# Two modulation vectors against 33.6 MB of weights: the weights become the stationary side of f32 products

## The chip, the core and the metric

One core of a Trainium2 chip runs the whole program, two transformer blocks on 256 tokens of width 2048. The metric is the device time in microseconds (us), the median of three runs; lower is better.

## What is computed

Only the start of the first block is touched by the change. Two vectors, `c` of the latent tokens and `c_ctx` of the context tokens, pass through silu and are multiplied by one matrix; the three parts of the result shift, scale and gate the block.

```python
c_act = jax.nn.silu(c)
cc_act = jax.nn.silu(c_ctx)
mod_lat = c_act @ w_ada[l] + b_ada[l]      # w_ada: 2048 x 6144, f32
mod_ctx = cc_act @ w_ada[l] + b_ada[l]
shift_l, scale_l, gate_l = jnp.split(mod_lat, 3, axis=-1)
u_l = rms_norm(h_lat, pre_w) * (1 + scale_l[:, None]) + shift_l[:, None]
u_c = rms_norm(h_ctx, pre_w) * (1 + scale_c) + shift_c
z_l, xbc_l, dt_l, qkv_l, b_l, a_l = _split_proj(u_l @ w_in)
```

Everything after that (two scans, gating, an output projection, then two layers of attention, convolution and MLP) is left as it is.

## The kernel before

The program is recorded by Python generators; a scheduler then orders the instructions of each engine, and each engine runs its own list strictly in that order. All activations stand feature-major: 128 features on the partitions, tokens along the free side.

Precision is the theme of the code. A product of two f32 numbers is made from float32r operands: `split` (lines 168 to 171) has ScalarE (ACT) write the rounded value `hi` and VectorE (DVE) the rest `lo`, and TensorE adds hi times hi, hi times lo and lo times hi. An operand that isn't split goes to TensorE as plain f32; the trace then shows two MATMUL records, each with a weight load (LDWEIGHTS), for one f32 product in the code.

The modulation runs first. `ada_prepare` (line 319) makes silu of both vectors (`cth`) and splits it (`cst`, 4 columns for each of 16 slices of 128 rows). `ada(m0, ...)` (line 331) makes four tiles of 128 outputs. For each of the 16 row slices it loads 128 x 512 weights (256 KB) on SyncE's DMA queue, splits them, and issues two products with `cst` as the stationary side (4 columns) and the weights moving (512 columns), once for `hi` and once for `lo`. At the end it copies the 4 x 512 result to SBUF, turns it with four transposes, and adds the parts and the bias into `modT` with two additions.

`block1_inputs` (line 390) drives this. For j = 0 to 3 it calls `ada` for four tiles of scale and then for four tiles of shift: eight calls, 128 weight tiles, 33.6 MB. The last third of `w_ada` (the gate) is done much later by `ada_gate`, in another way, from `cth`. Beside the calls, `along` (line 417) runs a side generator at every third step: during j = 0 it loads the 256 tokens of both sides and sums their squares on TensorE (16 f32 products of 512 columns); from j = 1 on it runs the first projections, 32 steps of 12 float32r products of 256 columns each. The eight steps of a j need the u tiles that its shift call completes, so the eight steps of j = 3 come after the last modulation. `small` (line 465) follows, with four transposes as its first work on TensorE.

The tile pools set how far loads run ahead: the split weights take their buffers from `RINGS` (line 1353), raw tiles from tags tok, kT and Am, `hi` from A and hs, `lo` from U and W.

Of the kernel before, what the change touches and what calls it, by code (L numbers as in the profile page):

```python
# [11 lines left out]
F32 = mybir.dt.float32  # L12
FR = mybir.dt.float32r
I32 = mybir.dt.int32
AF = mybir.ActivationFunctionType
ALU = mybir.AluOpType
# [6 lines left out]
NK = D // 128  # L23
# [8 lines left out]
class Kern:  # L32
# [286 lines left out]
    def ada_prepare(self):  # L319
        cv = self.cvec.rearrange("p (k t) -> p k t", t=2)  # L320
        th = self.lt([128, NK, 2], "cth")
        self.act(th, cv, AF.Tanh, scale=0.5)
        self.stt(th, th, 1.0, cv, ALU.add, ALU.mult)
        self.tsc(th, th, 0.5, ALU.mult)
        st = self.lt([128, NK, 4], "cst", FR)
        self.split(th, st[:, :, 0:2], st[:, :, 2:4])
        self.cst, self.cth, self.nada = st, th, 0
        self.modT = self.lt([128, 48, 2], "modT")
        self.wada = iter([self.a["w_ada"][i] for i in range(96)])

    def ada(self, m0, bank, rings):


        ps = self.pt([4, 512], bank)
        for kb in range(8):
            ap = next(self.wada)
            for kk in range(2):
                k = 2 * kb + kk
                i = self.nada = self.nada + 1
                raw, hi, lo = (self.m([128, 512], t[i % len(t)], dt) for t, dt in zip(rings, (F32, FR, FR)))  # L340
                self.nc.sync.dma_start(out=raw, in_=ap[:, kk * 512:kk * 512 + 512])
                self.split(raw, hi, lo)
                self.mm(ps, self.cst[:, k, :], hi, start=(k == 0), stop=False)
                self.mm(ps, self.cst[:, k, :], lo, start=False, stop=(k == NK - 1))
            if kb < 7:
                yield 1.4
        res = self.m([4, 512], "cc")
        self.act(res, ps)
        pm = self.pt([128, 4, 4], "pt")
        for t in range(4):  # L350
            self.transpose(pm[:, t, :], res[:, t * 128:t * 128 + 128])
        m = self.modT[:, m0:m0 + 4, :]
        self.tt(m, pm[:, :, 0:2], self.b_ada[:, m0:m0 + 4].unsqueeze(2).to_broadcast([128, 4, 2]), ALU.add)
        self.tt(m, m, pm[:, :, 2:4], ALU.add)
        yield 1.4

    def ada_gate(self, m0):
# [32 lines left out]
    def block1_inputs(self, early, got):  # L390

        nc = self.nc
        xs, r = [], []

        def first():
            ps = self.pt([128, 512], "pg")
            for j in range(4):
                if j < 2:
                    t = self.t8([128, 2, 4, T])
                    x = [t[:, 0], t[:, 1]]  # L400
                else:
                    x = [self.xt(), self.xt()]
                for s in range(2):
                    nc.sync.dma_start(out=x[s], in_=self.a["xc"][j, s])
                xs.append(x)
                yield
                for k in range(4 * j, 4 * j + 4):
                    sq = self.m([128, 2, T], "src")
                    for s in range(2):
                        self.act(sq[:, s], x[s][:, k % 4, :], AF.Square)  # L410
                    self.mm(ps, self.ones, sq.rearrange("p s t -> p (s t)"), start=(k == 0), stop=(k == NK - 1))
                yield
            q, x, t = (self.m([128, 512], "X"), self.m([128, 512], "g"), self.m([128, 512], "g"))
            self.rsqrt(q, ps, 1.0 / D, EPS, x, t)
            r.append(q)

        def along(m0, side):
            for i, dt in enumerate(self.ada(m0, "pc", RINGS)):
                if i % PUMP == 0:
                    next(side, None)  # L420
                yield dt

        self.u = [], []
        self.u_lat = self.pick(self.u[1])
        self.u_full = lambda k: (self.pick(self.u[0])(k), self.pick(self.u[1])(k))
        steps = []
        psc = self.lt([128, NK, 2], "psc")
        side = first()
        for j in range(4):
            yield from along(16 + 4 * j, side)  # L430
            if not j:
                for _ in side:
                    pass
                for i in range(0, len(early), 2):
                    ps = [self.acc([128, 1, 512]) if t == "acc" else self.pt([128, 1, 512], t) for t in early[i:i + 2]]
                    got += ps
                    steps.append(self.proj_steps(self.win, 2, self.u_full, 512, ps=ps, fine=True))
            m = slice(4 * j, 4 * j + 4)
            self.stt(psc[:, m, :], self.modT[:, 16 + 4 * j:20 + 4 * j, :], 1.0,
                     self.pre_w[:, m].unsqueeze(2).to_broadcast([128, 4, 2]), ALU.add, ALU.mult)  # L440
            for s in range(2):
                for k in range(4):
                    x, f = xs[j][s][:, k, :], 4 * j + k
                    self.stt(x, x, psc[:, f, s:s + 1], r[0][:, s * T:s * T + T], ALU.mult, ALU.mult)
            yield from along(4 * j, side)
            for _ in side:
                pass
            for s in range(2):
                u = self.t8([128, 2, 4, T], FR)
                for k in range(4):  # L450
                    x, f = xs[j][s][:, k, :], 4 * j + k
                    sh = self.modT[:, f, s:s + 1]
                    self.act(u[:, 0, k, :], x, AF.Identity, bias=sh)
                    self.stt(u[:, 1, k, :], x, sh, u[:, 0, k, :].bitcast(F32), ALU.add, ALU.subtract)
                self.u[s].append(u)
            side = (next(p) for p in steps for _ in range(4))
        for _ in side:
            pass
# [891 lines left out]
COPY = ("W", "W", "Am")  # L1350
EARLY = ("acc", "acc", "pA", "pg")
SHARE = 0
RINGS = (("tok", "tok", "kT", "tok", "Am"), ("A", "A", "hs"), ("U", "U", "W"))
SIDE0, SIDE, SIDK = 0, 2, (0,)
HEADS = range(0, 40, 5)
SHZ = 0
# [137 lines left out]
```

## Time and profile before

| | us |
|---|---|
| median of 3 runs | 3246.17 (3239.31 to 3249.16) |
| the profiled execution | 3253.82 |
| its span in the trace | 3252.0 |
| TensorE busy in the span | 3139.1 (97%) |
| VectorE busy | 2084.6 (64%) |
| ScalarE busy | 1538.7 (47%) |

A profile is of one execution. TensorE has two rows: PE is the matmuls, PEld the weight loads that run beside them. "Busy" is the union of an engine's instructions, and a matmul's record lasts longer than the time until the next can start, so a busy TensorE can still have room; the time that one matmul costs in a row of them is the distance from start to start. PEclk is the granted clock of TensorE, 1.00 for 2.4 GHz and 0.50 for 1.2 GHz. An average over 3.2 ms says nothing of the first 171 us, so the stretch is read by itself.

### The profile page before, as it was taken

What the parts mean: (1) busy time and instruction counts of PE and PEld (TensorE: products, weight loads), DVE (VectorE), ACT (ScalarE), POOL (GpSimd) and SP (SyncE); (2) the same over time, 40 slices, a digit from 0 to 9 for tenths busy, and PEclk for the clock granted to TensorE, in tenths of its full rate; (3) what the DMA queues carried; (4) which work ended last, traced back from release to release, by engine and by line L of the source; (5) the groups of instructions that cost most, each with busy time, mean ns of one, the idle gap of its engine ahead of it and who ended that gap; (6) DMA issues with size and microseconds to landing.
All of it is one profiled execution on the core that took longest, in us unless ns stands there. A gap on an engine that the chain in (4) does not pass through costs nothing.

```text
span 3252.0 us, 50361 instructions
## 1 busy us (share of the span) xinstructions
PE 3139.1 (97%) x19370; PEld 2730.0 (84%) x19370; DVE 2084.6 (64%) x3552; ACT 1538.7 (47%) x2290; POOL 530.5 (16%) x290
## 2 busy tenths in 40 slices
PE   7889999997989998999999999999999999999999
PEld 3589999987977887888888888888888888888888
DVE  7878988988756566555555554655765555555555
ACT  6654435453444455444444444444554544444443
POOL 0000000000002221322222222222213222222221
PEclk9999999998999999999999999999999999999999
DMA  9634432443764554565556565665546565555655
GB/s 319 229 105 118 125 102 86 114 112 117 249 236 153 166 180 136 186 187 188 182 189 187 188 185 185 188 189 159 179 159 186 185 189 185 185 188 186 191 184 181
DMA packets 217537, 565.75 MB, mean 174 GB/s; under 512 B 45808, under 2 KB 69856, under 8 KB 217296
## 3 DMA queue, kind: packets, MB, share of 16 engines
q1 hardware_dynamic: 214976, 555.72, 54.4%
q0 software_dynamic: 1456, 4.65, 0.4%
q8 instruction: 152, 2.49, 0.3%
q10 hardware_dynamic: 864, 2.16, 0.2%
q14 instruction: 89, 0.73, 0.1%
HBM read 552.83 MB, written 9.63 MB: 173 GB/s over the span
## 4 chain that ended last, share of the span: by engine, by line
PE 84%; DVE 5%; DMA 5%; ACT 2%; issue 1%; POOL 1%; SPq 0%; DVEq 0%; ACTq 0%; POOLq 0%
PE acc L146 76%; PE p_pc L146 3%; PE p_pg L146 2%; PE ps L146 2%; DVE lo L130 1%; DMA W<-w_ada 1%; DMA raw<-w_in 1%; ACT hi L143 1%; PE p_pA L146 1%; POOL lo L130 1%; DMA Am<-w_ada 1%; DMA A<-rows 1%; DVE t L133 1%; ACT t L143 0%; DMA t<-bias 0%
## 5 line engine op out<-in xcount | busy, mean ns | idle before, releaser
L146 PE MATMUL acc<-t,hi 128*128 128x512 f32 (+1 forms) x7552 | 2174.7, 356 | 18.7 <-ACT t L143 8.1
L146 PE MATMUL acc<-t,lo 128*128 128x256 f32 x6080 | 1659.3, 285 | 23.6 <-DVE lo L130 21.6
L143 ACT ACTIVATE hi<-raw 128x1024 fp32r<-128x1024 f32 x906 | 960.6, 1060 | 1337.3 <-PE acc L146 597.8
L146 PEld LDWEIGHTS acc<-t,hi 128*128 128x128 f32 x7552 | 1304.3, 190 | 232.6 <-DVE t L133 11.3
L146 PEld LDWEIGHTS acc<-t,lo 128*128 128x128 f32 x6080 | 1127.6, 190 | 51.3 <-DVE lo L130 26.8
L130 DVE TENSOR_TENSOR lo<-raw,hi 128x1024 fp32r<-128x1024 f32 x714 | 874.6, 1225 | 460.3 <-PE acc L146 383.6
L130 POOL TENSOR_TENSOR lo<-raw,hi 128x1024 fp32r<-128x1024 f32 x192 | 462.8, 2410 | 1874.9 <-PE acc L146 1621.8
L146 PE MATMUL acc<-c,hi 128*128 128x512 f32 x1280 | 459.5, 396 | 0.1
L146 PE MATMUL acc<-c,lo 128*128 128x256 f32 x1280 | 358.8, 280 | 0.0
L130 DVE TENSOR_TENSOR x<-x,acc 128x512 f32<-128x512 f32 x288 | 197.5, 686 | 215.5 <-PE acc L146 212.8
L146 PEld LDWEIGHTS acc<-c,hi 128*128 128x128 f32 x1280 | 240.4, 188 | 51.3 <-DVE t L130 0.4
L130 DVE TENSOR_TENSOR t<-t,acc 128x512 f32<-128x512 f32 x104 | 71.3, 687 | 296.4 <-ACT t L143 296.4
L146 PEld LDWEIGHTS acc<-c,lo 128*128 128x128 f32 x1280 | 241.5, 189 | 3.9
L133 DVE SCALAR_TENSOR_TENSOR cc<-src,featv,cc 128x248 f32<-128x248 f32 (+2 forms) x224 | 98.7, 470 | 0.3 <-ACT cc L143 0.2
L146 PE MATMUL acc<-hi,t 128*128 128x512 f32 x256 | 80.3, 393 | 0.0
L146 PE MATMUL ps<-t,t 128*128 128x128 f32 (+2 forms) x320 | 62.9, 340 | 10.7 <-ACT t L143 10.6
L133 DVE SCALAR_TENSOR_TENSOR t<-t,t 128x1024 f32<-128x1024 f32 (+2 forms) x68 | 62.4, 918 | 2.0
L146 PEld LDWEIGHTS ps<-t,t 128*128 128x128 f32 (+1 forms) x320 | 43.1, 180 | 23.5 <-ACT t L143 14.0
L143 ACT ACTIVATE t<-t 128x1024 f32<-128x1024 f32 (+1 forms) x56 | 59.3, 1059 | 6.4 <-DVE t L130 3.4
L130 DVE TENSOR_TENSOR t<-t,t 128x512 f32<-128x512 f32 (+2 forms) x64 | 60.4, 943 | 0.9
L725 POOL MEMSET W<- 64x256 f32 x16 | 4.9, 308 | 340.6 <-PE p_pg L146 268.0
L143 ACT ACTIVATE t<-acc 128x512 f32<-128x512 f32 x104 | 60.3, 582 | 0.0
(318 smaller groups left out, 2360.9 us busy)
## 6 DMA issues: line engine op xcount, KB each, us to landing
raw<-w_in SPq DMA_DIRECT2D x298, 512.0 KB, 3.8
raw<-w_up SPq DMA_DIRECT2D x256, 512.0 KB, 4.2
raw<-w_down SPq DMA_DIRECT2D x256, 512.0 KB, 3.8
raw<-w_out SPq DMA_DIRECT2D x96, 512.0 KB, 4.4
tok<-w_ada SPq DMA_DIRECT2D x77, 256.0 KB, 5.1
Am<-w_ada SPq DMA_DIRECT2D x57, 256.0 KB, 3.7
W<-w_ada SPq DMA_DIRECT2D x32, 256.0 KB, 3.4
kT<-w_ada SPq DMA_DIRECT2D x26, 256.0 KB, 5.9
```

Of the source, the lines that this page charges most:

```text
L130: return (eng or self.nc.vector).tensor_tensor(out=out, in0=in0, in1=in1, op=op)
L133: (eng or self.nc.vector).scalar_tensor_tensor(out=out, in0=in0, scalar=s, in1=in1, op0=op0, op1=op1)
L143: self.nc.scalar.activation(out=out, in_=in_, func=func, **kw)
L146: return self.nc.tensor.matmul(out, lhsT, rhs, start=start, stop=stop, skip_group_check=skip)
L725: nc.gpsimd.memset(W[jp], 0.0)
```

## The change

The weights are used as they arrive, in plain f32, as the stationary side: four products per weight tile, each with 128 columns of it, and the two vectors moving (2 columns). The result lies feature-major at once, in one PSUM bank of 128 x 4 x 2. The splits of the weights and of `cth`, the copy, the transposes and the second addition are gone. The raw tiles now rotate through one list of 23 buffers made of all the tags that raw, hi and lo had.

```diff
-        st = self.lt([128, NK, 4], "cst", FR)
-        self.split(th, st[:, :, 0:2], st[:, :, 2:4])
-        self.cst, self.cth, self.nada = st, th, 0
+        self.cth, self.nada = th, 0
...
-    def ada(self, m0, bank, rings):
+    def ada(self, m0):
-        ps = self.pt([4, 512], bank)
+        ps = self.pt([128, 4, 2], "pc")
         for kb in range(8):
             ap = next(self.wada)
             for kk in range(2):
                 k = 2 * kb + kk
-                i = self.nada = self.nada + 1
-                raw, hi, lo = (self.m([128, 512], t[i % len(t)], dt) for t, dt in zip(rings, (F32, FR, FR)))
+                raw = self.m([128, 512], RING[self.nada % len(RING)])
+                self.nada += 1
                 self.nc.sync.dma_start(out=raw, in_=ap[:, kk * 512:kk * 512 + 512])
-                self.split(raw, hi, lo)
-                self.mm(ps, self.cst[:, k, :], hi, start=(k == 0), stop=False)
-                self.mm(ps, self.cst[:, k, :], lo, start=False, stop=(k == NK - 1))
+                for t in range(4):
+                    self.mm(ps[:, t, :], raw[:, t * 128:t * 128 + 128], self.cth[:, k, :], start=k == 0 and t == 0,
+                            stop=k == NK - 1, skip=True)
             if kb < 7:
                 yield 1.4
-        res = self.m([4, 512], "cc")
-        self.act(res, ps)
-        pm = self.pt([128, 4, 4], "pt")
-        for t in range(4):
-            self.transpose(pm[:, t, :], res[:, t * 128:t * 128 + 128])
-        m = self.modT[:, m0:m0 + 4, :]
-        self.tt(m, pm[:, :, 0:2], self.b_ada[:, m0:m0 + 4].unsqueeze(2).to_broadcast([128, 4, 2]), ALU.add)
-        self.tt(m, m, pm[:, :, 2:4], ALU.add)
+        self.tt(self.modT[:, m0:m0 + 4, :], ps, self.b_ada[:, m0:m0 + 4].unsqueeze(2).to_broadcast([128, 4, 2]), ALU.add)
         yield 1.4
...
-RINGS = (("tok", "tok", "kT", "tok", "Am"), ("A", "A", "hs"), ("U", "U", "W"))
+RING = ("tok", "A", "U", "kT", "tok", "hs", "W", "A", "tok", "U", "Am", "kT", "tok", "A", "U", "tok", "hs", "W", "kT", "A",
+        "tok", "U", "Am")
```

TensorE's list in the third pair of calls, before. `p_pc` is the modulation's sum, A, hs and U, W the split weights; `p_pA` and `p_pg` are two of the early projections' sums, `t` their u tiles.

```order
L146 MATMUL p_pg_342<-t_240_901,hi_0_1187 128x256 x2
L146 MATMUL p_pg_342<-t_241_910,hi_0_1187 128x256 x2
L146 MATMUL p_pg_342<-t_240_901,lo_0_1188 128x256
L146 MATMUL p_pc_1108<-W_1205,cst 4x512
L146 MATMUL p_pc_1108<-A_1212,cst 4x512
L146 MATMUL p_pg_342<-t_241_910,lo_0_1188 128x256
L146 MATMUL p_pA_341<-t_240_901,hi_0_1187 128x256 x2
L146 MATMUL p_pc_1108<-U_1213,cst 4x512
L146 MATMUL p_pc_1108<-A_1220,cst 4x512
L146 MATMUL p_pA_341<-t_241_910,hi_0_1187 128x256 x2
L146 MATMUL p_pA_341<-t_240_901,lo_0_1188 128x256
L146 MATMUL p_pc_1108<-U_1221,cst 4x512
```

The scheduler wove single modulation products between the projection's. In the changed program, the same engine in the second pair of calls (an f32 product is one row here):

```order
L146 MATMUL p_pc_905<-cth,A_984 128x2 x4
L146 MATMUL p_pc_905<-cth,tok_990 128x2 x4
L146 MATMUL p_pc_905<-cth,U_996 128x2 x4
L146 MATMUL p_pc_905<-cth,Am_1002 128x2 x4
L146 MATMUL p_pc_905<-cth,tok_1008 128x2 x4
L146 MATMUL p_pc_905<-cth,A_1014 128x2 x4
L146 MATMUL p_pA_298<-t_104_738,hi_0_968 128x256 x2
L146 MATMUL p_pA_298<-t_105_747,hi_0_968 128x256 x2
L146 MATMUL p_pA_298<-t_104_738,lo_0_969 128x256
L146 MATMUL p_pA_298<-t_105_747,lo_0_969 128x256
L146 MATMUL p_pg_299<-t_104_738,hi_0_968 128x256 x2
L146 MATMUL p_pg_299<-t_105_747,hi_0_968 128x256 x2
```

Now the list alternates between six weight tiles (24 products of two columns) and one step of 12 projection products.

VectorE's list in the first half of the modulation, before:

```order
L130 TENSOR_TENSOR U_561<-kT_559,A_560 128x512
L130 TENSOR_TENSOR W_569<-tok_567,hs_568 128x512
L130 TENSOR_TENSOR modT<-p_pt_483,featv 128x8
L130 TENSOR_TENSOR U_577<-Am_575,A_576 128x512
L130 TENSOR_TENSOR U_585<-tok_583,A_584 128x512
L130 TENSOR_TENSOR W_605<-tok_603,hs_604 128x512
L130 TENSOR_TENSOR U_613<-kT_611,A_612 128x512
L130 TENSOR_TENSOR modT<-modT,p_pt_483 128x8
```

and in the changed program, from the first to the third pair of calls:

```order
L133 SCALAR_TENSOR_TENSOR t_66_407<-t_6_118,modT,t_66_407 128x256 x4
L133 SCALAR_TENSOR_TENSOR t_67_416<-t_6_118,modT,t_67_416 128x256 x4
L130 TENSOR_TENSOR modT<-p_pc_425,featv 128x8
L133 SCALAR_TENSOR_TENSOR psc<-modT,featv 128x8
L133 SCALAR_TENSOR_TENSOR t_23_209<-t_23_209,psc,X_281 128x256 x8
L130 TENSOR_TENSOR lo_0_772<-raw_769,hi_0_771 128x1024
L130 TENSOR_TENSOR modT<-p_pc_574,featv 128x8
L133 SCALAR_TENSOR_TENSOR t_104_738<-t_23_209,modT,t_104_738 128x256 x4
```

The splits stood between all other work of VectorE; now only the u tiles, the bias additions and the projection weights' splits are left there.

## Rows read from the trace of the kernel before

**Rows 1.** The page, head and busy time (share of the span, instructions)
```profile
span 3252.0 us, 50361 instructions
PE 3139.1 (97%) x19370; PEld 2730.0 (84%) x19370; DVE 2084.6 (64%) x3552; ACT 1538.7 (47%) x2290; POOL 530.5 (16%) x290
```

**Rows 2.** Windows: stretch, its length, engines' busy us (instructions), PEclk, DMA share, GB/s
```profile
0.00:171.00 171.00, 143.17 (x709) 79.69 (x709) 127.29 (x244) 113.81 (x219) 1.22 (x6) 0.93 0.78 263
```

**Rows 3.** The chain of waits, five pieces of 89 to 171 us: start, us, what
```profile
89.53 6.23 DMA tok<-w_ada
...
120.76 1.30 DVE U L130 x2
...
157.16 0.18 DVE modT L130
...
160.46 1.48 PE acc L146 x12
...
170.58 0.39 PE p_pt L150 x4
```

**Rows 4.** Timeline of modulation steps: start, us, engine, line, what [idle before, releaser]
```profile
6.30 0.63 ACT L143 ACTIVATE A<-tok 128x512 fp32r<-128x512 f32 x1 [1.36 <-DMA tok<-w_ada]
...
15.60 0.63 PE L146 MATMUL p_pc<-U,cst 128*4 128x512 f32 x1
...
90.03 0.68 DVE L130 TENSOR_TENSOR U<-tok,A 128x512 fp32r<-128x512 f32 x1
...
153.70 0.40 PE L146 MATMUL p_pc<-U,cst 128*4 128x512 f32 x1
153.93 0.39 PE L146 MATMUL p_pc<-hs,cst 128*4 128x512 f32 x1
```

**Rows 5.** The tile p_pc over the whole span: duration ns min/median/max, first and last start
```profile
L146 PE MATMUL p_pc<-gV,gK x96: 271/275/580, 454.0 to 832.0; 128*128 128x128 f32 x96
```

**Rows 6.** Timeline at 1117 us, two f32 products with one moving column (line 1321's helper)
```profile
1117.76 0.52 PEld L146 LDWEIGHTS ps<-consts,t 1*128 1x128 f32 x4 [0.35 <-PE acc L146]
1117.76 0.60 PE L146 MATMUL ps<-consts,t 1*128 1x1 f32 x4
```

**Rows 7.** Groups of weight loads by form: count | busy us, mean ns of one | idle before
```profile
L146 PEld LDWEIGHTS ps<-consts,t 1*128 1x128 f32 x8 | 1.0, 185 | 0.7 <-PE acc L146 0.7
...
L150 PEld LDWEIGHTS p_pt<-consts,cc 4*128 4x128 f32 x32 | 2.6, 136 | 4.1 <-ACT cc L143 3.2 <-ACT A L143 0.5
```

**Rows 8.** Timeline of weight loads at 215 us, granted clock 0.50
```profile
214.94 0.97 PEld L146 LDWEIGHTS acc<-t,hi 128*128 128x128 f32 x4
215.79 0.54 PEld L146 LDWEIGHTS acc<-t,lo 128*128 128x128 f32 x2
```

**Rows 9.** Timeline of TensorE: sums of squares, then projections, both at clock 1.00
```profile
22.69 5.75 PE L146 MATMUL p_pg<-src,consts 128*128 128x512 f32 x12
27.88 0.80 PE L146 MATMUL p_pc<-A,cst 128*4 128x512 f32 x1
...
164.66 0.64 PE L146 MATMUL acc<-t,hi 128*128 128x256 f32 x4
165.14 0.40 PE L146 MATMUL acc<-t,lo 128*128 128x256 f32 x2
```

**Rows 10.** Windows with a steady clock: columns as in Rows 2
```profile
17.69:38.17 20.48, 18.98 (x58) 7.05 (x56) 9.06 (x14) 15.76 (x39) 0.00 (x0) 1.00 1.04 398
38.17:45.00 6.83, 6.02 (x14) 1.22 (x15) 6.83 (x15) 5.06 (x10) 0.00 (x0) 0.50 1.04 393
45.00:51.83 6.83, 3.37 (x13) 0.70 (x12) 6.76 (x12) 3.58 (x7) 0.00 (x0) 1.00 0.77 256
754.97:768.63 13.66, 9.12 (x44) 7.12 (x42) 11.09 (x32) 3.02 (x10) 0.61 (x2) 0.50 0.14 21
```

**Rows 11.** DMA queues from 0 to 160 us: packets, MB, share of 16 engines
```profile
q1 hardware_dynamic: 21312, 43.75, 79.6%
```

**Rows 12.** Timeline of weight loads of the transposes that end a modulation call
```profile
35.87 0.32 PEld L150 LDWEIGHTS p_pt<-consts,cc 4*128 4x128 f32 x4 [0.76 <-ACT cc L143]
```

More of the change, by code (lines that the diff above doesn't have):

```diff
@@ L417, in along @@
         def along(m0, side):
-            for i, dt in enumerate(self.ada(m0, "pc", RINGS)):
+            for i, dt in enumerate(self.ada(m0)):
                 if i % PUMP == 0:
```

## The prediction, made before the changed kernel ran

> **What bounds the kernel now.** I read the page's head first: TensorE is busy 97% of 3252.0 us [rows 1], but that average belongs to the projections and the MLP. So I cut the span where the change ends. From 0 to 171 us TensorE is busy 143.17 us, VectorE 127.29, ScalarE 113.81, and DMA moves 263 GB/s [rows 2]. The chain of waits shows what limits the first stretch: no one engine, but a relay. It waits for a weight tile's DMA (6.23 us at 89.53), for VectorE's `lo` (1.30 us at 120.76), then ends through `modT` at 157.16, the last u tiles, the projections from 160.46, and the first transposes of `small` at 170.58 [rows 3]. I take that 170.6 us as the end of the stage; all later work waits behind it in TensorE's list, so a stage that ends later by some time should end the program later by as much.
>
> **The change, part by part.**
> *Gone from ScalarE and VectorE:* 128 roundings of 0.63 us and 128 rests of 0.68 us [rows 4], 81 and 87 us, and in each of eight calls a copy, four transposes and an addition. This shortens the path only if TensorE or DMA doesn't take its place.
> *Gone from TensorE:* 256 products of 512 columns, 0.23 us from start to start (153.70, 153.93) [rows 4], 59 us. The two vectors' own split is a few tenths; I give it nothing.
> *Added to TensorE:* 128 tiles times 4 products, 512 f32 products of two moving columns. Each is two load-and-matmul pairs: the scan's `p_pc<-gV,gK` is 8 heads x 3 steps x 2 directions, 48 products in the code, and has 96 records [rows 5]. So 1024 pairs. What is one pair with a 128-column load and almost no stream worth? The nearest row is an f32 product with one moving column: four loads in 0.52 us and their matmuls in 0.60 [rows 6], with 0.185 us for one load [rows 7], so (0.52 - 0.185)/3 = 0.112 us from start to start. I take that: the load sets the pace. 1024 x 0.112 = 115 us against the 59 that went.
> A rule would make that dearer. The Trainium skill (FP8 and Floating Point Precision, section TensorE Precision Notes) says that true f32 takes four passes through the array; with a load for each pass, 2048 pairs would be 229 us. The trace has two records per product [rows 5], so the rule, if it holds, is inside those records and already in their price; I don't use it.
> *The clock is the larger question.* At granted clock 0.50, loads of 128 columns start 0.213 us apart (four from 214.94 to 215.79) [rows 8], and there 1024 pairs cost 218 us. Which level will hold? From 38.17 to 45.00 the weight loads, of four columns, are 1.22 us of 6.83, the streams of 512 columns fill PE to 6.02, and the clock returns from 0.50 to 1.00 at the end; from 45.00 to 51.83 the streams thin out to 3.37 us and it falls afterwards; from 754.97 to 768.63 loads fill 7.12 of 13.66 us beside short, broken-up matmuls, and the clock stays at 0.50 all the way [rows 10]. So here it follows streamed columns and does not rise on loads. No row shows loads nearly alone, which the change makes, so both levels stay as bounds. I take the low one: a pair streams two columns where before a product streamed 512.
> *Staying on TensorE in the stage:* 32 records for the squares, 0.43 us each (twelve from 22.69 to 27.88) [rows 9], 13.8 us, 27.5 at half clock, which I take, since they are spread among the pairs of the first two calls. And 384 projection matmuls at 0.12 (four from 164.66 to 165.14) [rows 9], 46 us, or 0.213 at half clock. Of these the last 96 come after the last modulation, without pairs between: 11.5 us at full clock. The other 288 lie in bundles of 12 between 24 products of pairs: 34.6 to 61.3 us; I take 48, since bundles can lift the clock for moments.
> *DMA:* 43.75 MB by 160 us [rows 11] at the 398 GB/s of 17.69 to 38.17 [rows 10] is 110 us. With 23 raw buffers it runs ahead of TensorE and costs nothing; it would show again only if TensorE needed under 110 us. On SyncE's queue the loads keep their number.
> *Ends:* the first tile is there at 6.3 us [rows 4] and needs no rounding. From the last `modT` to flowing projections before took 160.46 - 157.16 = 3.3 us [rows 3], one addition of about 0.2 less now: 3.1.
> **Sum at half clock:** 6.3 + 218 + 27.5 + 48 + 11.5 + 3.1 = 314.4 us, against 170.6: 144 us later. The scheduler also reorders the rest of block 1 in detail; I give that +-10 us and no sign. On the profiled execution's 3253.8 us (span 3252.0 and 1.8 around it) this makes 3398; that execution lay 7.7 us over the median of the runs, so for the median 3246.2 + 144 = **3390**.
>
> **The rivals.**
> *Full clock.* The loads count, or bundles suffice. 115 + 13.8 + 46 + 9.4 = 184, and about 6 for a slow start (a modulation product still took 0.63 us at 15.60, against 0.40 at 153.70 [rows 4]): 190, 19.6 us later, 3266. For it: TensorE never idles. The Trainium skill (TensorE: Matmul & The Clock Gate, section Why this matters for your kernels) advises to keep TensorE continuously busy to leave the throttled state; by that rule a gapless row of pairs would run at full clock. The stretch at 754.97 speaks against counting loads, as far as it goes. The price would be that of this rival.
> *Clock in between.* Each projection bundle lifts the clock and the following pairs keep it for a while, or two columns count for more than two. Half of the pairs at each price: 166 + 20.7 + 48 + 9.4 + 6 = 250, 80 us later, 3326.
> *Faster: the loads overlap better than in the nearest row.* A transpose's loads, of 128 columns too, are (0.32 - 0.136)/3 = 0.061 us apart [rows 7, 12]. At that price 62 + 13.8 + 46 + 9.4 + 6 = 137, 33 us sooner, 3213, and DMA's 110 close behind. It decides below (170.6 - 59.8 - 15.4)/1024 = 0.093 us a pair. For it: VectorE and ScalarE, which held the relay, are free. Against it: the f32 row has the same kind of load as the change's, the transpose has not, and it gives 0.112.
>
> **How the numbers follow.** Half clock 0.66, in between 0.13, full clock 0.15, faster 0.05, the rest 0.01. The likeliest case has its own range: all matmuls at full clock with the pairs at half, 6.3 + 218 + 13.8 + 46 + 3.1 = 287, is 117 later, 3363; all at half but the last 96, 328, is 157 later, 3403, and with the reordering 3413. Two in ten may be left out, so the range must reach down through the middle case into the full-clock one: **3260 to 3413**. It leaves out about half of the full-clock case, the faster one and a little at the top. What a measurement can tell here is 0.3%, some 10 us. The first three cases are all slower by more: 0.92, with 0.03 for a full-clock case that wins some back and stays within; 0.05 faster.
>
> **What would show it.** Right: 1024 matmul records on `p_pc` from `cth`, two moving columns each, 0.21 us apart in rows; PEclk near 0.5 through most of the first 300 us; TensorE without gaps there; VectorE and ScalarE nearly idle; DMA in pauses; `small`'s transposes near 315 us; the stages after as long as before. Wrong: pairs 0.11 us apart and the transposes near 190, then it was the clock; pairs under 0.093 us, or more than two records per product, then it was the price of a load; a stage of 315 us with a program not later by as much, then it was the slack behind it.

## The result, and the profile after

| | before | changed |
|---|---|---|
| median, us | 3246.93 (3239.31 to 3249.16, 4 runs) | 3371.83 (3362.16 to 3374.38, 4 runs) |
| ratio, with its 95% interval | | 1.0372 (1.0356 to 1.0388) |
| the profiled execution, us | 3253.82 | 3370.05 |
| its span, us | 3252.0 | 3368.2 |

The change makes the program 3.7% slower. The forecast had the sign, the place and the mechanism; it took the loss for 144 us where the stage lost 120.

The head of the page after the change answers to [rows 1]: TensorE is busy 146 us longer, VectorE 79 and ScalarE 74 us less. The row PEclk, from the same page, is the granted clock of TensorE in 40 slices of 84 us, in tenths (9 is 90% or more).

```profile
span 3368.2 us, 51341 instructions
PE 3285.2 (98%) x20106; PEld 2926.4 (87%) x20106; DVE 2005.2 (60%) x3415; ACT 1464.7 (43%) x2153; POOL 530.5 (16%) x290
...
PEclk7558999999899999999999999999999999999999
```

The same row of the kernel before, in slices of 81 us:

```profile
PEclk9999999998999999999999999999999999999999
```

The first four slices hold the modulation, and after the change they stand at 7, 5, 5 and 8 tenths. To see that nothing else moved, the span is cut at the same events in both kernels: the end of the modulation's stage (first transposes of `small`), the work up to the next use of `modT` (`gp`), and the rest. The windows of the changed kernel (columns as in [rows 2]):

```profile
0.00:291.00 291.00, 283.02 (x1446) 267.63 (x1447) 50.71 (x110) 39.25 (x82) 1.22 (x6) 0.64 0.45 155
291.00:1081.00 790.00, 746.18 (x6021) 716.78 (x6020) 660.51 (x1692) 360.78 (x753) 8.49 (x32) 0.97 0.44 135
1081.00:3368.20 2287.20, 2255.96 (x12643) 1941.99 (x12641) 1293.99 (x1614) 1064.68 (x1320) 520.75 (x252) 1.00 0.53 181
```

And the second and third window of the kernel before; its first one is [rows 2]:

```profile
171.00:958.00 787.00, 737.80 (x6021) 709.22 (x6022) 661.53 (x1694) 360.91 (x753) 8.45 (x32) 0.98 0.45 136
958.00:3252.00 2294.00, 2258.14 (x12644) 1941.11 (x12642) 1295.82 (x1615) 1063.94 (x1319) 520.86 (x252) 1.00 0.57 180
```

The first stage grew by 120 us, the second by 3, and the third shrank by 7, which makes the 116 us between the spans. In the first stage TensorE is busy 283 of 291 us where it was 143 of 171. DMA moves 155 GB/s where it moved 263, at TensorE's pace now. The clock of 0.64 in the first row flatters: the first change of the clock on record is at 29 us, and what lies before it is shown as 1.00, though loads are 0.21 us apart there as at half clock. From 29 us on it is 0.60:

```profile
29.00:291.00 262.00, 262.00 (x1373) 250.79 (x1374) 50.08 (x106) 33.61 (x68) 0.00 (x0) 0.60 0.39 135
```

Windows of the runs below begin, where the clock matters, behind the first change on record.

The chain of waits of the changed kernel (start, us, what), to be held against [rows 3]: the relay of DMA, rounding and rest is gone, and the chain is TensorE alone, 48 pairs and then 12 projection products, over and over, until the transposes of `small` at 290.34, which were at 170.58.

```profile
119.09 2.77 PE acc L146 x12
121.86 10.03 PE p_pc L146 x48
...
228.86 10.03 PE p_pc L146 x48
238.89 2.77 PE acc L146 x12
...
290.34 0.39 PE p_pt L150 x4
```

What one pair costs is read in the timeline of weight loads (start, us, engine, line, what, how many). One piece at half clock and one that begins at full clock:

```profile
82.19 1.83 PEld L146 LDWEIGHTS p_pc<-cth,Am 128*128 128x128 f32 x8
83.90 1.83 PEld L146 LDWEIGHTS p_pc<-cth,kT 128*128 128x128 f32 x8
85.61 1.83 PEld L146 LDWEIGHTS p_pc<-cth,tok 128*128 128x128 f32 x8
...
135.58 0.97 PEld L146 LDWEIGHTS p_pc<-cth,kT 128*128 128x128 f32 x8
136.47 0.97 PEld L146 LDWEIGHTS p_pc<-cth,tok 128*128 128x128 f32 x8
137.36 0.97 PEld L146 LDWEIGHTS p_pc<-cth,A 128*128 128x128 f32 x8
138.26 1.54 PEld L146 LDWEIGHTS p_pc<-cth,U 128*128 128x128 f32 x8
```

Eight pairs take 1.71 us in the first piece (83.90 - 82.19), 0.213 each, and 0.89 in the second, 0.112 each. Both prices are those of the prediction. The granted clock belongs to them (windows of the changed kernel):

```profile
118.08:131.73 13.65, 13.65 (x65) 13.65 (x66) 2.53 (x5) 1.06 (x1) 0.00 (x0) 0.50 0.49 166
135.15:138.56 3.41, 3.41 (x32) 3.41 (x32) 0.00 (x0) 0.00 (x0) 0.00 (x0) 1.00 0.35 114
278.51:289.00 10.49, 10.49 (x90) 10.49 (x89) 4.59 (x8) 3.95 (x5) 0.00 (x0) 1.00 0.27 88
```

In the first of these, pairs with one bundle of 12 projection products among them, TensorE loads and multiplies without a gap for 13.65 us, and stays at 0.50 (1.2 GHz). In the second, which follows a bundle of 12 projection products, it is at 1.00 (2.4 GHz); only pairs run in it, and right behind it the loads slow down (the last row of the timeline: eight in 1.54 us). The third is the tail, projections alone, at full clock.

### The profile page after: what moved, and what is told of

It is laid out like the page before. It is cut to its first block, busy times and chain, and to the rows that moved or that the text cites. A ratio compares the mean times of both kernels' runs of the same rounds, so it can differ in the third digit from the quotient of the medians.

```text
span 3368.2 us, 51341 instructions
## 1 busy us (share of the span) xinstructions
PE 3285.2 (98%) x20106; PEld 2926.4 (87%) x20106; DVE 2005.2 (60%) x3415; ACT 1464.7 (43%) x2153; POOL 530.5 (16%) x290
## 4 chain that ended last, share of the span: by engine, by line
PE 88%; DVE 5%; DMA 5%; issue 1%; ACT 1%; SPq 0%; POOL 0%; DVEq 0%; ACTq 0%; POOLq 0%
PE acc L146 75%; PE p_pc L146 7%; PE p_pg L146 3%; PE ps L146 2%; DVE lo L130 1%; DMA W<-w_ada 1%; PE p_pA L146 1%; DMA raw<-w_in 1%; DMA Am<-w_ada 1%; DMA A<-rows 0%; ACT hi L143 0%; PE p_pt L150 0%; DVE t L133 0%; PE p_pg L150 0%; DVE g L133 0%
## 5 line engine op out<-in xcount | busy, mean ns | idle before, releaser
L146 PEld LDWEIGHTS acc<-t,hi 128*128 128x128 f32 x7552 | 1313.0, 192 | 221.0 <-DVE t L133 11.6
L130 DVE TENSOR_TENSOR t<-t,acc 128x512 f32<-128x512 f32 x104 | 71.3, 687 | 294.8 <-ACT t L143 294.8
L146 PEld LDWEIGHTS p_pc<-cth,tok 128*128 128x128 f32 x272 | 55.4, 298 | 11.0 <-issue 11.0
L146 PE MATMUL p_pc<-cth,tok 128*128 128x2 f32 x272 | 55.0, 323 | 7.9 <-DMA tok<-w_ada 7.9
L146 PEld LDWEIGHTS ps<-t,t 128*128 128x128 f32 (+1 forms) x320 | 41.6, 175 | 22.2 <-ACT t L143 12.6
```

What stands on the lines that cost most here:

```text
L130: return (eng or self.nc.vector).tensor_tensor(out=out, in0=in0, in1=in1, op=op)
L146: return self.nc.tensor.matmul(out, lhsT, rhs, start=start, stop=stop, skip_group_check=skip)
```

## The experiments

Each kernel is compared with runs of the kernel before on the same chip. Two theories stand first. **A**: a pair costs its 128-column load, 0.112 us at full clock, and the clock is lost because two streamed columns per load don't hold it. **B**: the price is the load's, and the pace of 0.213 belongs to this order of loads and short matmuls whatever the stream is. They part when the stream is made wider and the loads are left alone.

### More moving columns, the same loads: wide128, wide64, wide32

The two vectors of slice k stand in a long row of all slices, and the product takes 128, 64 or 32 columns from there on. Only the first two of the result are read.

```diff
-        ps = self.pt([128, 4, 2], "pc")
+        ps = self.pt([128, 4, 64], "pc")
...
-                    self.mm(ps[:, t, :], raw[:, t * 128:t * 128 + 128], self.cth[:, k, :], start=k == 0 and t == 0,
+                    self.mm(ps[:, t, :], raw[:, t * 128:t * 128 + 128], self.cwide[:, 2 * k:2 * k + 64], start=k == 0 and t == 0,
```

> The changed kernel with 128 moving columns instead of 2: the two vectors of the row slice and behind them 126 columns that belong to the other slices and are not used. Loads and pairs stay 1024. Theory A (the granted clock follows the columns that are streamed, weight loads do not hold it): PEclk near 1.00 after the start, pairs 0.11 us apart, the first transposes of the later step near 190 us (180 to 200) instead of 290, the program about 100 us faster than the changed kernel, 3255 to 3275. Rival B (a load of plain f32 weights costs 0.21 us by itself and the clock is a bystander): the stage stays at 290 us or grows, 3370 or more.

> As before with 64 moving columns. Theory A: the stream fills about half of each load's time at full clock; once a run of the squares or of projections has lifted the clock it should stay up, so a somewhat later rise than with 128 columns and then the same pairs of 0.11 us: transposes at 185 to 210 us, 3255 to 3290. Rival B: 290 us, 3370.

> As before with 32 moving columns, sixteen times those of the change. Theory A: the stream fills a quarter of a load's time; PEclk stays mostly at 0.50, somewhat more often up than in the change: transposes at 250 to 290 us, 3330 to 3370. Rival A2 (any real stream behind each load is enough): as with 128 columns, 190 us. Rival B: 290 us.

| | stage ends, us | median, us | ratio to before (95%) |
|---|---|---|---|
| changed, 2 columns | 290.3 | 3371.83 | 1.0372 (1.0356 to 1.0388) |
| 32 columns | 261.8 | 3331.47 | 1.0237 (1.0219 to 1.0256) |
| 64 columns | 186.3 | 3264.28 | 1.0043 (1.0026 to 1.006) |
| 128 columns | 186.5 | 3265.26 | 1.0041 (1.0028 to 1.0054) |

The window of wide64 from 30 us to the end of its stage, and its loads (timeline):

```profile
30.00:187.00 157.00, 157.00 (x1312) 151.06 (x1311) 50.23 (x106) 32.61 (x66) 0.00 (x0) 1.00 0.64 222
```

```profile
100.34 0.97 PEld L146 LDWEIGHTS p_pc<-cth,tok 128*128 128x128 f32 x8
101.24 0.97 PEld L146 LDWEIGHTS p_pc<-cth,A 128*128 128x128 f32 x8
102.13 0.97 PEld L146 LDWEIGHTS p_pc<-cth,U 128*128 128x128 f32 x8
```

The window of wide32, from just behind its first change of the clock on record, at 54 us, to the end of the stage:

```profile
55.00:262.00 207.00, 207.00 (x1271) 203.04 (x1270) 47.16 (x101) 27.43 (x56) 0.00 (x0) 0.70 0.39 129
```

With the same 1024 loads, 62 columns of unused work per product make the stage 104 us shorter: the clock is 1.00 throughout, and the pairs are 0.112 apart. With 32 columns it is 0.70 over the last 207 us of the stage, and the stage lies between. B falls. 128 columns are worth no more than 64: the load sets the pace and hides the stream. (512 columns of f32 take 0.43 us [rows 9], so 128 are an estimated 0.108 us, just inside the load's 0.112.) What is left against the kernel before, 186.3 against 170.6, is mainly the dearer load: the pairs take 115.9 us in wide64 (summed from start to start of TensorE's matmuls, so with their waits), the split products 95.2 before, and the squares 3.6 more than before; the transposes and their waits, 7.4 us, are gone. That is the prediction's full-clock rival, which put the stage at 190 and the loss at 19.6 us; wide64 loses 15.8 in the stage and 12.9 between the medians.

### Columns of zeros: zeros64

```diff
+        self.nought = self.lt([128, 64], "nought")
+        self.nc.vector.memset(self.nought, 0.0)
...
-                    self.mm(ps[:, t, :], raw[:, t * 128:t * 128 + 128], self.cth[:, k, :], start=k == 0 and t == 0,
+                    self.mm(ps[:, t, :], raw[:, t * 128:t * 128 + 128], self.nought, start=k == 0 and t == 0,
```

> The changed kernel with 64 moving columns that are all zero, so the product with the modulation weights is left out and the modulation is its bias alone. Theory A as it stands (streamed columns hold the clock, whatever they hold): as with 64 real columns, pairs 0.112 us apart, transposes at 186 us, about 3265. Rival: the clock follows work that switches, zeros do not count: mostly 0.50, transposes at 260 to 290 us, 3330 to 3370.

The window from 30 us to the end of the stage:

```profile
30.00:193.00 163.00, 163.00 (x1365) 157.13 (x1365) 49.99 (x105) 32.01 (x66) 0.00 (x0) 1.00 0.65 214
```

Zeros hold the clock as numbers do: 1.00 for 163 us, and the rival, mostly 0.50, falls. The stage ends at 192.9, 6.6 us after that of wide64. The loads show where: they are 0.213 us apart until 30 us, in wide64 only until 17. Whether zeros are slower to lift the clock, or that was chance, one execution can't say: the first rise on record lies at 16 us in wide128 too, but at 29 in the changed kernel and at 54 in wide32. The run's time of 3272.89 us is a single one as well, against a median of 3255.20 before.

### The sides exchanged: f32moving

If A holds, the clock also returns when the f32 weights move, 512 columns for a load of two.

```diff
-                for t in range(4):
-                    self.mm(ps[:, t, :], raw[:, t * 128:t * 128 + 128], self.cth[:, k, :], start=k == 0 and t == 0,
-                            stop=k == NK - 1, skip=True)
+                self.mm(ps, self.cth[:, k, :], raw, start=k == 0, stop=k == NK - 1)
...
+        res = self.m([2, 512], "cc")
+        self.act(res, ps)
+        pm = self.pt([128, 4, 2], "pt")
+        for t in range(4):
+            self.transpose(pm[:, t, :], res[:, t * 128:t * 128 + 128])
```

> The changed kernel with the sides exchanged: the two vectors stationary (2 columns), the plain f32 weights moving (512 columns), no splits, a copy and four transposes at the end of each call as before the change. 256 records of 0.43 us, 110 us of TensorE where the change has 1024 pairs. Theory A: the streams keep PEclk at 1.00, the stage ends at 180 to 200 us, 3255 to 3275, the same as with 128 columns although there are a quarter of the loads and only 2 columns in each. Rival B (loads are the cost): shorter than with 128 columns, below 171 us.

Window and timeline of its matmuls:

```profile
30.00:197.00 167.00, 165.09 (x671) 69.99 (x670) 48.27 (x102) 37.04 (x74) 0.00 (x0) 1.00 0.59 206
```

```profile
101.36 1.02 PE L146 MATMUL p_pc<-tok,cth 128*2 128x512 f32 x2
102.22 1.02 PE L146 MATMUL p_pc<-U,cth 128*2 128x512 f32 x2
```

Two records take 0.86 us from start to start (101.36, 102.22), 0.43 each; 256 of them are 110 us, nearly the 115 of 1024 loads at full clock. The clock is 1.00, the stage ends at 196.7, the median is 3273.15, the ratio 1.0059 (1.0039 to 1.0078). So for these tiles plain f32 has much the same price on either side of the array, as long as the clock holds. What doubled that price in the changed kernel was the clock.

### Half the loads: onepass64

To see what a load is worth, the weights are rounded to float32r by ScalarE and used with 64 moving columns, so that a product is one pair. The rests of both sides are left out, so part of the precision of the two other kernels is missing.

```diff
-                raw = self.m([128, 512], RING[self.nada % len(RING)])
+                raw = self.m([128, 512], RAWS[self.nada % len(RAWS)])
+                hi = self.m([128, 512], HIS[self.nada % len(HIS)], FR)
...
+                self.act(hi, raw)
...
-                    self.mm(ps[:, t, :], raw[:, t * 128:t * 128 + 128], self.cth[:, k, :], start=k == 0 and t == 0,
+                    self.mm(ps[:, t, :], hi[:, t * 128:t * 128 + 128], self.cwide[:, 2 * k:2 * k + 64], start=k == 0 and t == 0,
```

> 64 moving columns, and both sides rounded to float32r (ScalarE rounds each weight tile, as before the change; the rests of weights and vectors are left out, so the modulation is less exact). One record per product instead of two: 512 loads. If the load is the price at full clock: 512 x 0.112 = 57 us of TensorE instead of 115, the sum is 57 + 11 + 46 + 9 = 123 us, ScalarE 81 us of roundings and DMA 110 us beside it, so transposes at 125 to 145 us and 3200 to 3225. If something else than the loads holds the stage (DMA, the projections), 160 to 186 us and 3240 to 3265.

```profile
0.00:151.00 151.00, 134.48 (x935) 120.96 (x936) 51.07 (x112) 107.68 (x211) 1.22 (x6) 0.90 0.85 299
```

512 loads instead of 1024: the pairs take 71.3 us against 115.9 in wide64, waits included, and neighbouring pairs are again 0.112 us apart (median). So the load is the price, but the stage ends at 150.2, between the two ranges that were expected, and the median, 3235.49, lies between theirs; the ratio is 0.9947 (0.9927 to 0.9967). It is the only kernel of this study that beats the one before, and it computes less. TensorE is idle for 16 of the 151 us of this window, ScalarE busy for 108 and DMA at 0.85, and waits for the weights' DMA (`tok`) make 13.9% of the chain of waits up to 150 us, 7.1% before the change: the limit moves back towards the relay of [rows 3].

### A few slices in f32, the rest split: mix4 and mix7

Since f32 with weights moving runs at full clock, it could relieve VectorE in the kernel before. Of 16 slices of each call, 4 (mix4) or 7 (mix7: odd k below 15) skip the split:

```diff
...
+                if k % 4 == 2:
+                    self.mm(ps[0:2], self.cth[:, k, :], raw, start=False, stop=False, skip=True)
+                    continue
...
```

> The kernel before the change, but 4 of the 16 row slices of each call go to TensorE as plain f32 moving weights against the unsplit vectors, into the same sum; no split for them. TensorE: 96 tiles at 0.46 and 32 at 0.86 us, 72 us instead of 59; VectorE and ScalarE lose 32 splits each, 22 and 20 us. If the stage before was a relay with VectorE as its busiest part, transposes at 150 to 162 us instead of 170.6, 3230 to 3242. If it was TensorE or DMA, no gain: 168 to 180, 3250 to 3260.

> The same with 7 of the 16 row slices in plain f32: TensorE 72 x 0.46 + 56 x 0.86 = 81 us for the modulation, 141 with squares and projections; VectorE 38 us less than before the change. Relay: transposes at 150 to 160 us, about as with 4 slices, 3228 to 3242. TensorE bound: 165 to 175, no gain.

The first stage of mix4, against [rows 2]:

```profile
0.00:167.00 167.00, 151.04 (x709) 75.06 (x710) 109.18 (x212) 97.32 (x187) 1.22 (x6) 0.98 0.79 269
```

Both miss: the relay reading was too simple. VectorE lost 18 us of work and the stage of mix4 only 4 (166.5, between the two ranges that were expected); TensorE's own work rose by 8, and DMA, at 269 GB/s against 263, hardly sped up. The chain of waits moved to TensorE: up to the end of the stage its modulation products (`p_pc`) make 41.6% of the chain in mix4, 21.2% before. The program isn't faster: 1.0015 (1.0006 to 1.0023). By `gp` it is 7 us behind the kernel before (965.1 against 957.9), so the work between, which the edit doesn't touch, took 11 us more. The scheduler had put the rest of block 1 in another order. It had in wide64 too, where that work took no longer, so what costs the 11 us stays open. mix7 ends its stage at 176.4, ratio 1.006 (1.0047 to 1.0072).

### Some rests on GpSimd: pool4 and pool3

The other way to relieve VectorE: GpSimd subtracts for every fourth (pool4) or third slice (pool3: k % 3 == 1).

```diff
-                self.split(raw, hi, lo)
+                self.split(raw, hi, lo, self.nc.gpsimd if k % 4 == 2 else None)
```

> The kernel before the change, with the rest (lo) of every fourth row slice of the modulation's weights made on GpSimd instead of VectorE. TensorE keeps its 121 us; VectorE loses 32 x 0.68 = 22 us, GpSimd, idle in this stage, gets 32 at about 1.2 us. If VectorE's place in the relay held the stage: transposes at 150 to 163 us, 3235 to 3248 beside 3255 of before. If the two engines hinder each other or the slower GpSimd is waited for in TensorE's order: 168 to 180 us, 3250 to 3265.

> The same with every third row slice (5 of 16): VectorE loses 27 us, GpSimd gets 48 us. Relay theory: 148 to 162 us, 3233 to 3248. Otherwise as with every fourth, 168 to 182.

The stage ends at 172.1 in pool4 and 175.6 in pool3, the ratios are 1.002 (1.0009 to 1.0031) and 1.0055 (1.0042 to 1.0067): no gain. What became of VectorE's relief is seen in the tile U of pool4 (duration in ns, least, median and most, then first and last start):

```profile
L130 DVE TENSOR_TENSOR U<-tok,A x38: 674/679/1792, 7.1 to 150.2; 128x512 fp32r<-128x512 f32 x38
L130 POOL TENSOR_TENSOR U<-tok,A x13: 1266/1352/1604, 12.6 to 147.0; 128x512 fp32r<-128x512 f32 x13
```

and in its timeline near the end of the modulation, first GpSimd's rows, then VectorE's:

```profile
143.64 1.29 POOL L130 TENSOR_TENSOR W<-Am,hs 128x512 fp32r<-128x512 f32 x1 [4.31 <-ACT hs L143]
146.99 1.39 POOL L130 TENSOR_TENSOR U<-tok,A 128x512 fp32r<-128x512 f32 x1 [2.05 <-ACT A L143]
```

```profile
144.12 1.37 DVE L130 TENSOR_TENSOR U<-tok,A 128x512 fp32r<-128x512 f32 x1 [0.82 <-ACT A L143]
...
147.22 1.70 DVE L130 TENSOR_TENSOR W<-kT,hs 128x512 fp32r<-128x512 f32 x1
```

Both subtractions on VectorE start while GpSimd subtracts, and end 0.56 us (145.49 after 144.93) and 0.54 us (148.92 after 148.38) after GpSimd's, close to their whole usual 0.68: they stood still until then. Of the 26 that start so in pool4, 21 end 0.55 us after GpSimd's; the other five take their usual 0.68, while a GpSimd subtraction stretches to 3.6 or 3.9 us and is the one that waits. The Trainium skill (SBUF — State Buffer, section SBUF: two separate sides) says that VectorE, with two inputs in SBUF, and GpSimd exclude each other for a whole instruction. Trace and rule agree, and the four subtractions that pool4 takes from VectorE in each call are paid back in waits: VectorE's busy time to the end of the stage rose from 127.3 us [rows 2] to 133.5. How much of the missing gain this accounts for stays open, since mix4, without such waits, gained only 4 us in the stage.

## Why the prediction was right, and where its size was off

**The price of a pair.** Right at both levels: 0.112 and 0.213 us forecast, 0.112 and 0.213 measured, with two records for a product, 1024 in all. Luck had a part in it. The row behind 0.112 has loads of a single row (1 x 128) [rows 6], and the one behind 0.213 has projection matmuls of 256 columns behind its loads [rows 8, 9], so it couldn't tell the load's pace from the stream's. That pairs with two columns keep these paces, only the changed kernel shows. The Trainium skill's four passes for f32 (FP8 and Floating Point Precision, TensorE Precision Notes), which the prediction set aside, show as no pairs beyond two records for a product. They can lie inside the records: in f32moving an f32 product of 512 columns takes 0.86 us, where a float32r product before took 0.23 [rows 4].

**The clock.** The mechanism was right, and wide64 shows it: give the streams columns, and 104 of the 120 us come back with not one load fewer. The rows that it was read from were not enough by themselves: those of [rows 10] fit as well a clock that follows TensorE's busy time (6.02 of 6.83 us before a rise, 3.37 before a fall, 9.12 of 13.66 where it stays low). The changed kernel parts the two, with TensorE busy for 262 us at a mean of 0.60. And the step "I take the low one", for all pairs, was too simple. The sum's terms, each measured from start to start of TensorE's matmuls over the first stage:

| term, us | forecast | measured |
|---|---|---|
| first tile | 6.3 | 7.9 |
| pairs | 218 | 184.1 |
| squares | 27.5 | 27.0 |
| projections | 48 + 11.5 | 71.3 |
| end | 3.1 | within the rows above |
| sum | 314.4 | 290.3 |

*Pairs* are the term that was mis-sized, by 34 us. Of 988 distances between neighbouring pairs, 277 are about 0.11 us and 669 about 0.21. A bundle of projections (or, in the first two calls, of squares) can be followed by a rise of the clock, and the pairs behind it go at the cheaper price until it falls again (135.15 to 138.56, above). Of the 18 bundles from 109 us to the last pair six were, three stood at the upper level already, and nine left it at the lower; what parts them stays open. That is the mechanism of the rival "clock in between", which put half of the pairs at each price, 166 us, and had a chance of 0.13. The truth, 29% at the cheaper price, lies between the two cases, for this term somewhat nearer to the rival.

*Projections* were mis-sized the other way, by 12 us: "bundles can lift the clock for moments" made the 288 products before the tail 48 us, and they took 59.6, near the 61.3 of half clock. A bundle that is followed by a rise has itself mostly run at 0.50. The tail was right: its 96 products took 11.6 us. *Squares* ran at half clock as taken. The *end* needed no time of its own: 24 products of earlier bundles stood behind the last pair and filled it.

The two errors partly cancel, so that the stage, at 290.3, is nearer to the forecast's 314.4 than to the rival's 250, and the median of 3371.83 lies inside the likeliest case's own range.

**The rest.** "A stage that ends later by some time should end the program later by as much": 119.8 in the stage, 116.2 in the span. The 10 us set aside for reordering held here (+3 and -7). DMA, VectorE and ScalarE cost nothing, as taken. The full-clock rival was worked out rightly and needs only the 62 unused columns to come true; its support, the Trainium skill's advice to keep TensorE continuously busy (TensorE: Matmul & The Clock Gate, Why this matters for your kernels), doesn't carry over to this work: TensorE was busy all of the 262 us from 29 to 291 at a mean clock of 0.60. The faster rival would have needed pairs below 0.093 us; none of the runs shows a row of such pairs at that pace.

## What to carry to other kernels

When one side of a product has a few columns, price a pair by its weight load, at both levels of the clock, and ask whether the streams are wide enough to hold the upper one: a TensorE that is busy with loads alone can run at half clock. If the thin side must move, let it move with unused columns up to what the load hides anyway (here 64 cost as little as 128, and 104 us less than 2); otherwise keep it stationary and move the wide side. Taking work off an engine that shares a relay with others, as mix4 and pool4 did, gave back little here, and the work behind, in another order, can take that too.

## What the runs showed that was not expected

- Columns of zeros hold the clock like any others: 1.00 from 30 to 193 us in zeros64, in one execution.
- Between 2 and 64 columns the time follows the share of it that the clock stands at its upper level: with 32, 442 distances between pairs are near 0.11 us and 503 near 0.21; with 64 it is up from 17 us to the end of the stage.
- A weight load that starts before the stream ahead of it is through hides where that stream's time goes: from load to load the squares of the changed kernel seem to take 16.8 us, from matmul to matmul 27.0. Terms of a sum are better taken from matmul to matmul.
- VectorE's subtraction of 0.68 us took up to 1.79 when GpSimd was subtracting, so VectorE, with 32 subtractions fewer, was busy longer than before.
- Work that an edit doesn't touch varies by up to 20 us between these kernels: from the modulation's end to `gp` the kernel before took 787.4 us, wide64 785.8, the changed one 790.5, wide32 779.3 and mix4 798.6, one execution each. Whether its order does it is not shown. So of the 37 us between the spans of the changed kernel and wide32 only 28.5 lie in the stage, and 11 in this work.
